# A mixer layer: column-wise small inverse, preparation in three steps, and elementwise work queued behind evacuations

## The chip, the cores and the metric

The kernel runs on one core of a Trainium2 chip. The metric is the device time of one execution in microseconds. Before the change the median of three runs was 3375.29 us (3373.78 to 3380.63).

A core has five engines that work side by side, each through its own queue in order. PE multiplies matrices; PEld is its loading of weights. DVE and POOL do elementwise work, ACT does activation functions and copies, and SP only issues DMAs here. An instruction that waits for another engine's result holds up everything behind it in its own queue.

## The reference

One layer works on 256 latent tokens and 256 context tokens of width 2048, all in float32: a SwiGLU block on both, a token mixer, and a second SwiGLU block on the latent tokens alone, each followed by a residual sum and a layer norm. The change touches the mixer. Half of its width is an RWKV-7 recurrence, with 16 heads of 64 channels, run forwards and backwards; the other half is a gated MLP over chunks of 128 tokens:

```
def token_mixer(h_x, h_c, ...):
    p_x, p_c = h_x @ w_in, h_c @ w_in                       # 2048 -> 3 * 1024 + 256 + 2 * 1024
    r, k, v, w_lo, a_lo, g_lo = split(xs)                   # xs: token-shifted projections
    w     = -softplus(-(w0[d] + tanh(w_lo) @ w_up[d])) - 0.5
    iclr  = sigmoid(a0[d] + a_lo @ a_up[d])
    k_d   = k * (1 + (iclr - 1) * k_a)
    decay = exp(-exp(w))
    # per head and direction d, over tokens t (context first, then latent):
    S_t = S_{t-1} (diag(w_t) + a_t^T b_t) + v_t^T k_t,   y_t = S_t r_t
    out = (group_norm(y) + bonus) * g                       # RWKV half
    gm  = u * (W_s layer_norm(v) + b)                       # gated MLP half
    return concat([out, gm]) @ w_out
```

## The kernel before

Large products are made of three matmuls each (`mm3`, lines 313 to 316), with weights and activations split into a high and a low part. For the weights `wsplit` (line 293) does this: SP loads 512 KB into one of three buffers `raw`, ACT rounds it to `whi` (line 302), and DVE or POOL subtracts to get `wlo` (line 305). There are four buffers of each part.

The recurrence is cut into chunks of 64 tokens. A **unit** is one pair of heads in one direction: 8 pairs times 2 directions make 16 units, numbered 0 to 15. Even units (d = 0) run forwards, odd ones backwards. A unit passes through three chains of steps:

- `begin` (line 1103): for even units a prologue, then `prep` (line 712). From the projections it makes the decays (`pz`, `zp`, the scan `pf`, the exponentials `e`, `ei`), the scaled keys `bk` and receptances `ar`, `ac`, the chunk matrices `aa` by matmuls `px` and a masked copy, transposes `pt` and products `pak`.
- `inverse` (line 858): each 64 x 64 triangular chunk matrix is inverted. `small_inverse` (line 825) collects its 16 x 16 diagonal blocks into `a16` on DVE (line 833), writes them to DRAM (`scr`), and reads them back spread over the partitions as `abc` (1 MB, line 839). `small_steps` (line 845) then makes 15 substitution steps on DVE, each a product with `abc` (line 852) and a reduction (line 853). Four rounds of small matmuls (`pX`, `pR`, twice each) with evacuations on DVE or ACT join the blocks to the whole inverse `R`.
- `finish` (line 1121): `solve` makes `pu`, `pg`, `pq`, and then walks over the 8 chunks: `pS` on PE, the new state `S` on DVE (line 1011), and so on, with outputs `py` and `y`. Backward units add the group norm (`pgn`, line 1072) and the gate (`gup` loaded from DRAM, `pgt`, `epilogue`).

`together` (line 1132) runs `finish` of unit u, `inverse` of u + 1 and `begin` of u + 2 side by side. Every `yield` ends a step; after each round of steps `burst` takes some **project work** from a queue: the large products of the projections of later units (`pp`), of the gated MLP (`pgv`, `pu` with `h` as input) and of the output projection (`pwo`). `pace` sets how much: what is left, over the units left, over `SLOTS`. One step of project work is three matmuls of 256 columns. A scheduler that keeps each engine's program order as the priority, and a model of when inputs are ready, fixes the order of every queue when the program is built; `tc.issue_after(ins)` makes instructions stand behind `ins` on their engine.

Of the kernel before, what the change touches and what calls it, by code (L numbers as in the profile page):

```python
# [38 lines left out]
SLOTS = 13  # L39
# [14 lines left out]
def tile_layer(ctx: ExitStack, tc: tile.TileContext, x, c, ctx_in, c_ctx, w_ada, b_ada, ln_g, ln_b,  # L54
# [89 lines left out]
    mb = const.tile([P, 4], F32, name="mb")  # L144
    for b in range(4):
        nc.vector.tensor_tensor(mb[:, b:b + 1], (bit1 if b >= 2 else bit0)[32], (bit1 if b % 2 else bit0)[16], op=ALU.mult)
# [144 lines left out]


    def wsplit(src, n, by_col=False):

        _, a, b = src.shape
        raw = wp.tile([P, a, b], F32, tag="raw", name="raw", bufs=RAWB)
        nc.sync.dma_start(raw, src)
        parts = []
        for i in range(n):
            r = raw[:, :, b // n * i:b // n * (i + 1)] if by_col else raw[:, a // n * i:a // n * (i + 1), :]  # L300
            hi = wp.tile(list(r.shape), F32R, tag="whi", name="whi", bufs=HIB)
            nc.scalar.copy(hi, r)  # L302
            lo = wp.tile(list(r.shape), F32R, tag="wlo", name="wlo", bufs=HIB)
            turn[0] += 1
            (nc.gpsimd if turn[1] and turn[0] % turn[1] == 0 else nc.vector).tensor_tensor(lo, r, hi.bitcast(F32), op=ALU.subtract)  # L305
            parts.append((hi, lo))
        return parts
# [393 lines left out]

    gl = const.tile([P, T], F32, name="gl")
# [9 lines left out]
    def prep(t, d, k, r, kk, vt, ups, kdx, s):  # L712
# [12 lines left out]
        nc.scalar.activation(ic, pa, AF.Tanh, scale=0.5, bias=a0c)  # L725
        nb = pre("nb")
        nc.vector.scalar_tensor_tensor(nb, ic, 1.0, kk, op0=ALU.add, op1=ALU.mult)

        nc.vector.tensor_reduce(zp[:, :, 0], zp[:, :, 1:L // 2 + 1], axis=AX.X, op=ALU.add, negate=True)
        pf = pre("pf", (P, NCH, L + 1))  # L730
        nc.vector.tensor_tensor_scan(fl(pf), fl(m65), fl(zp), 0.0, op0=ALU.mult, op1=ALU.add)
# [4 lines left out]
        nc.scalar.activation(fl(ei), fl(pf), AF.Exp, scale=-sgn)  # L736
# [3 lines left out]
        wn = own("wn", (P, NCH), bufs=3)  # L740
        if d == 0:
            nc.vector.tensor_tensor(wn[:, 0:7], e[:, 0:7, last], ei[:, 1:8, first], op=ALU.mult)
        else:
            nc.vector.tensor_tensor(wn[:, 1:8], e[:, 1:8, last], ei[:, 0:7, first], op=ALU.mult)
            nc.vector.tensor_tensor(wn[:, 0:1], e[:, 0:1, last], ei[:, 7:8, first], op=ALU.mult)
        ei = ei[:, :, 1:L + 1] if d == 0 else ei[:, :, 0:L]
        ar = pre("ar", (P, 2, 4, L))
# [4 lines left out]
        bk = [pre(f"bk{q}", (P, 4, 2, L)) for q in range(2)]  # L752
        nbv, eiv = (z.rearrange("p (g q) t -> p g q t", q=2) for z in (c64(nb), ei))
        for q in range(2):
            nc.vector.scalar_tensor_tensor(bk[q][:, :, q, :], nbv[:, :, q, :], -0.5, eiv[:, :, q, :], op0=ALU.mult, op1=ALU.mult)
        nc.vector.tensor_tensor(ar[:, 1], c64(r), ecur[:, 4:8], op=ALU.mult)

        kd = pre("kd")
        nc.vector.tensor_scalar(kd, ic, -1.0, kac, op0=ALU.add, op1=ALU.mult)
        nc.vector.scalar_tensor_tensor(kd, kd, 1.0, k, op0=ALU.add, op1=ALU.mult)  # L760
        kdv = c64(kd).rearrange("p (g q) t -> p g q t", q=2)
        for q in range(2):
            nc.gpsimd.tensor_tensor(bk[q][:, :, 1 - q, :], kdv[:, :, q, :], eiv[:, :, q, :], op=ALU.mult)
# [4 lines left out]
        for _ in range(3):  # L768
            yield
# [5 lines left out]
        for half in (1, 0):  # L775
# [16 lines left out]
            for h in range(2):  # L792
# [6 lines left out]
                nc.vector.tensor_tensor(aa[:, :, h, 2 * half:2 * half + 2], pa, mk[0], op=ALU.mult)  # L799
# [9 lines left out]
        for q in range(2):  # L809
# [3 lines left out]
            nc.scalar.copy(fl(bkt[:, q]), pt)  # L813
# [8 lines left out]
        nc.scalar.copy(rhs[:, :, :, 0, :], pt.rearrange("p (g h c) -> p g h c", g=4, h=2))  # L822
        s.update(wn=wn, rt=rt, aa=aa, arm=arm, rhs=rhs, bkt=bkt)

    def small_inverse(d, s):


        a16 = own("a16", (P, 8, 16))
        for b in range(4):
            for q in range(2):  # L830
                qs = slice(64 * q, 64 * q + 64)
                aq = s["aa"][qs, q].rearrange("p h g t -> p (h g) t")
# [3 lines left out]
        scr = dr.tile([P, 128], F32, tag="scr", name="scr")  # L836
        nc.sync.dma_start(scr, fl(a16))
        abc = own("abc", (P, 16, 8, 16))
        nc.sync.dma_start(abc.rearrange("p s j t -> p (s j t)"),
                            scr.rearrange("(g s) c -> g (s c)", g=8).unsqueeze(1).to_broadcast([8, 16, 2048]))  # L840
        return small_steps(d, s, abc)

    behind = [None]

    def small_steps(d, s, abc):
        x = own("x16", (P, 8, 16), bufs=2)
        nc.scalar.copy(x, i16.unsqueeze(1).to_broadcast([P, 8, 16]))
        sub = own("a16", (P, 8, 16))
        for i in (range(1, 16) if d == 0 else range(14, -1, -1)):
            r = slice(0, i + 1) if d == 0 else slice(i, 16)  # L850
            with tc.issue_after(behind[0].ins) if behind[0] is not None and i in (1, 14) else nullcontext():
# [6 lines left out]
    def inverse(d, s):  # L858

        aa = s["aa"]  # L860
        for _ in range(3):
            yield
        yield from s["small"]

        R1 = own("R1", (P, 8, 32))
        nc.vector.tensor_tensor(R1.rearrange("p j (b t) -> p j b t", t=16), s["x16"].unsqueeze(2).to_broadcast([P, 8, 2, 16]),
                                mh[:, 0, :].unsqueeze(1).unsqueeze(3).to_broadcast([P, 8, 2, 16]), op=ALU.mult)
        Rt = own("Rt", (P, 8, 32))
        nc.vector.transpose(Rt, R1)
# [8 lines left out]
        nc.vector.tensor_tensor(Z, pX[:, 0:256].rearrange("p (i t) -> p i t", t=32),  # L878
# [23 lines left out]
        for q in range(2):  # L902
            sb = slice(64 * q + fb, 64 * q + fb + 32)
            pz = pX[sb, 0:256].rearrange("p (i t) -> p i t", t=32)
            if q:
                nc.scalar.copy(Z[sb], pz)
# [8 lines left out]
        for q in range(2):  # L915
            sa = slice(64 * q + fa, 64 * q + fa + 32)
            pz = pR[sa, 0:256].rearrange("p (i t) -> p i t", t=32)
            if q:
                nc.scalar.copy(R[sa, :, fb:fb + 32], pz)
# [4 lines left out]
    def solve(d, s, vt, y):  # L924
# [7 lines left out]
        for half in range(2):  # L932
# [12 lines left out]
            nc.scalar.copy(uv[1][64:128, g2], puv[64:128, :, :, 0, :])  # L945
# [588 lines left out]
```

## Time and profile before

| | us |
|---|---|
| median of three runs | 3375.29 |
| the profiled execution | 3370.43 |
| its span, first to last instruction | 3368.7 |
| PE busy in the span | 3202.2 |
| DVE busy | 2163.8 |
| ACT busy | 1255.9 |
| POOL busy | 436.7 |

The page gives for each engine the time in which it was busy. Its strip of 40 slices shows PE at 9 tenths and more nearly everywhere, except between about 1600 and 2610 us, where slices stand at 7 to 9 and the clock that PE was granted lies at 8 or 9 tenths. The 16 units run in that part, from 1727 to 2572 us. A busy PE there isn't a PE at its peak: matmuls are pipelined, and each counts as busy until its result is out.

### The profile page before, as it was taken

The numbers are of one execution on the slowest core, as the hardware profiler recorded it, in microseconds if no ns is written. First come the engines' busy times: TensorE is split into PE (matmuls) and PEld (weight loads), VectorE is DVE, ScalarE is ACT, GpSimd is POOL, SyncE is SP. The second block draws the span as 40 slices with busy tenths as digits, with TensorE's granted clock in tenths as the row PEclk, the third lists the DMA queues.
The fourth block names the chain that finished last, engine by engine and source line by source line (L and its number), as shares of the span: only waits on it lengthen the run. The fifth ranks groups of instructions, "written<-read, shape, count | busy, mean of one in ns | idle before, by whom it ended". The sixth has DMA issues, their size and how long they took to land. (4 is left out here: it accounts for less than half of the span.)

```text
span 3368.7 us, 55611 instructions
## 1 busy us (share of the span) xinstructions
PE 3202.2 (95%) x21224; PEld 2548.5 (76%) x21224; DVE 2163.8 (64%) x4425; ACT 1255.9 (37%) x2205; POOL 436.7 (13%) x393
## 2 busy tenths in 40 slices
PE   8999999999999999999798989888889999999997
PEld 4556877777877887888787777777678888888886
DVE  3345677967566566443967777877677756656567
ACT  2321222222222222222564454444333554444443
POOL 2100000000000000000553232323223000000003
PEclk9999999999999999999898899998899999999999
DMA  9866464756656556333354253444453665555554
GB/s 302 266 198 204 142 187 150 218 176 221 194 159 225 159 181 201 120 95 106 119 162 116 73 123 88 108 100 107 124 117 124 221 209 193 190 191 188 188 189 148
DMA packets 546387, 554.35 MB, mean 165 GB/s; under 512 B 24207, under 2 KB 399156, under 8 KB 544072
## 3 DMA queue, kind: packets, MB, share of 16 engines
q1 hardware_dynamic: 545672, 550.61, 53.3%
q8 instruction: 167, 2.74, 0.3%
q14 instruction: 100, 0.82, 0.1%
q0 software_dynamic: 384, 0.17, 0.0%
q10 hardware_dynamic: 64, 0.02, 0.0%
HBM read 543.35 MB, written 7.35 MB: 163 GB/s over the span
## 5 line engine op out<-in xcount | busy, mean ns | idle before, releaser
L302 ACT CAST whi<-raw 128x512 fp32r<-128x512 f32 (+1 forms) x1366 | 840.1, 618 | 1717.9 <-PE po L315 356.0
L305 DVE TENSOR_TENSOR wlo<-raw,whi 128x512 fp32r<-128x512 f32 (+1 forms) x1188 | 833.4, 704 | 630.8 <-ACT whi L302 621.1
L305 POOL TENSOR_TENSOR wlo<-raw,whi 128x512 fp32r<-128x512 f32 x178 | 242.5, 1365 | 2565.2 <-ACT whi L302 2518.2
L314 PE MATMUL po<-ahi,whi 128*128 128x512 f32 (+1 forms) x768 | 292.4, 381 | 2.8 <-DVE X L420 2.2
L316 PE MATMUL po<-ahi,wlo 128*128 128x512 f32 (+1 forms) x768 | 290.4, 378 | 4.6 <-DVE wlo L305 4.6
L315 PE MATMUL po<-alo,whi 128*128 128x512 f32 (+1 forms) x768 | 291.7, 380 | 0.0
L314 PE MATMUL pgate<-h,whi 128*128 128x512 f32 x704 | 277.9, 395 | 1.8 <-ACT h L310 1.2
L314 PE MATMUL pup<-h,whi 128*128 128x512 f32 x704 | 278.0, 395 | 0.9 <-ACT whi L302 0.9
L316 PE MATMUL pup<-h,wlo 128*128 128x512 f32 x704 | 275.2, 391 | 1.0 <-DVE wlo L305 0.9
L316 PE MATMUL pgate<-h,wlo 128*128 128x512 f32 x704 | 275.1, 391 | 0.8 <-DVE wlo L305 0.6
L315 PE MATMUL pgate<-h,whi 128*128 128x512 f32 x704 | 274.7, 390 | 0.0
L315 PE MATMUL pup<-h,whi 128*128 128x512 f32 x704 | 274.5, 390 | 0.0
L420 DVE SCALAR_TENSOR_TENSOR X<-po,modc,X 128x256 f32<-128x256 f32 x352 | 155.0, 478 | 154.6 <-PE po L316 149.4
L277 DVE SCALAR_TENSOR_TENSOR vt<-xk,wa,vt 128x512 f32<-128x512 f32 x256 | 186.9, 746 | 28.7 <-DMA xk<-in_w_ada_dram 26.7
L277 DVE SCALAR_TENSOR_TENSOR vt<-xv,wa,vt 128x512 f32<-128x512 f32 x224 | 163.5, 746 | 24.1 <-DMA xv<-in_w_ada_dram 22.6
L314 PEld LDWEIGHTS po<-ahi,whi 128*128 128x128 f32 x768 | 145.4, 189 | 42.4 <-issue 7.0
L314 PEld LDWEIGHTS pgate<-h,whi 128*128 128x128 f32 x704 | 132.1, 188 | 53.5 <-ACT whi L302 11.5
L315 PEld LDWEIGHTS po<-alo,whi 128*128 128x128 f32 x768 | 145.6, 190 | 35.0 <-issue 7.5
L316 PEld LDWEIGHTS po<-ahi,wlo 128*128 128x128 f32 x768 | 145.5, 189 | 34.2 <-DVE wlo L305 5.3
L314 PEld LDWEIGHTS pup<-h,whi 128*128 128x128 f32 x704 | 132.2, 188 | 51.7 <-ACT whi L302 13.2
L314 PE MATMUL pp<-h,whi 128*128 128x256 f32 (+1 forms) x448 | 164.6, 367 | 3.3 <-ACT whi L302 2.3
L316 PE MATMUL pp<-h,wlo 128*128 128x256 f32 (+1 forms) x448 | 157.0, 351 | 7.2 <-DVE wlo L305 4.3
(389 smaller groups left out, 6323.9 us busy)
## 6 DMA issues: line engine op xcount, KB each, us to landing
raw<-in_ffn_b_wi_dram SPq DMA_DIRECT2D x176, 512.0 KB
raw<-in_ffn_a_wi_dram SPq DMA_DIRECT2D x156, 512.0 KB
xv<-in_w_ada_dram SPq DMA_DIRECT2D x256, 256.0 KB
xk<-in_w_ada_dram SPq DMA_DIRECT2D x256, 256.0 KB
raw<-in_w_in_dram SPq DMA_DIRECT2D x110, 512.0 KB
raw<-in_ffn_a_wo_dram SPq DMA_DIRECT2D x96, 512.0 KB
raw<-in_ffn_b_wo_dram SPq DMA_DIRECT2D x88, 512.0 KB
abc<-scr SPq DMA_DIRECT2D x16, 1024.0 KB
```

What stands on the lines that cost most here:

```text
L277: nc.vector.scalar_tensor_tensor(acc[v], raw, csil[:, kt, v:v + 1], acc[v], op0=ALU.mult, op1=ALU.add)
L302: nc.scalar.copy(hi, r)
L305: (nc.gpsimd if turn[1] and turn[0] % turn[1] == 0 else nc.vector).tensor_tensor(lo, r, hi.bitcast(F32), op=ALU.subtract)
L314: nc.tensor.matmul(o, wh, ah, start=start, stop=False)
L315: nc.tensor.matmul(o, wh, al, start=False, stop=False)
L316: nc.tensor.matmul(o, wl, ah, start=False, stop=stop)
L420: nc.vector.scalar_tensor_tensor(xs, po[:, sl], gc[:, d:d + 1], xs, op0=ALU.mult, op1=ALU.add)
```

## The change

Outside the mixer one constant (`mb`) goes, and the rest of the program stays. In the mixer:

- The 16 x 16 blocks are no longer collected on DVE. Eight DMAs per unit write them from `aa` to `scr`, in runs of 16 numbers, and `abc` is read inside `prep` instead of after the round.
- The substitution goes by columns: the product reads `abc` in runs of neighbours, without the diagonal, and `sub` starts as the identity on ACT.
- `prep` is cut into three steps, with the DVE's part of each behind the last evacuation noted in `urgent`; `kd` is made before `bk`, and POOL takes `bk` before `ar` and `ac`.
- `inverse` starts one step earlier and has one more step between the transposed block and `pX`. `begin` comes before `inverse` in each round.
- `whi` and `wlo` on ACT and DVE stand behind the evacuations of the round before.
- Both norms become two operations over all groups; that of the gated MLP moves into `gmlp_u`; the group norm has one more step, and `gup` is loaded in the fifth step of `solve`.
- `SLOTS` is 12 instead of 13.

```diff
-SLOTS = 13
+SLOTS = 12
...
+    def queued(ins):
+        return tc.issue_after(ins.ins) if ins is not None else nullcontext()
...
-            nc.scalar.copy(hi, r)
+            with queued(before[1]):
+                nc.scalar.copy(hi, r)
...
-            (nc.gpsimd if turn[1] and turn[0] % turn[1] == 0 else nc.vector).tensor_tensor(lo, r, hi.bitcast(F32), op=ALU.subtract)
+            with queued(before[0]):
+                (nc.gpsimd if turn[1] and turn[0] % turn[1] == 0 else nc.vector).tensor_tensor(lo, r, hi.bitcast(F32), op=ALU.subtract)
...
+    def behind():
+
+        return queued(urgent[0])
...
+        with behind():
+            nc.vector.tensor_reduce(zp[:, :, 0], zp[:, :, 1:L // 2 + 1], axis=AX.X, op=ALU.add, negate=True)
+            nc.vector.tensor_tensor_scan(fl(pf), fl(m65), fl(zp), 0.0, op0=ALU.mult, op1=ALU.add)
+        yield
...
+        with behind():
+
+            nc.vector.tensor_scalar(kd, ic, -1.0, kac, op0=ALU.add, op1=ALU.mult)
+            nc.vector.scalar_tensor_tensor(kd, kd, 1.0, k, op0=ALU.add, op1=ALU.mult)
+            nc.vector.scalar_tensor_tensor(nb, ic, 1.0, kk, op0=ALU.add, op1=ALU.mult)
+        yield
...
+        scr = dr.tile([P, 128], F32, tag="scr", name="scr")
+        for q in range(2):
+            for b in range(4):
+                rows = slice(64 * q + 16 * b, 64 * q + 16 * b + 16)
+                nc.sync.dma_start(scr[rows, :].rearrange("p (j t) -> p j t", t=16),
+                                  aa[rows, q].rearrange("p h g t -> p (h g) t")[:, :, 16 * b:16 * b + 16])
         yield
...
-                nc.vector.scalar_tensor_tensor(a16[qs], aq[:, :, 16 * b:16 * b + 16], mb[qs, b:b + 1],
-                                               a16[qs] if b else i16[qs].unsqueeze(1).to_broadcast([64, 8, 16]),
-                                               op0=ALU.mult, op1=ALU.add)
...
-                nc.vector.tensor_tensor(sub[:, :, r], x[:, :, r], abc[:, r, :, i].rearrange("p s j -> p j s"), op=ALU.mult)
-            nc.vector.tensor_reduce(x[:, :, i], sub[:, :, r], axis=AX.X, op=ALU.add)
-            if i % 4 == 0:
+            with behind():
+                nc.vector.tensor_tensor(sub[:, :, lo:hi], x[:, :, lo:hi], s["abc"][:, i, :, lo:hi], op=ALU.mult)
+                nc.vector.tensor_reduce(x[:, :, i], sub[:, :, r], axis=AX.X, op=ALU.add)
+            if n % 4 == 3:
                 yield
...
+        nc.vector.transpose(R1, Rt)
+        yield
         yield
         pX = ps_v("pX")
...
-                nc.vector.scalar_tensor_tensor(Sn, pS[:, 0:64], wn[:, cc:cc + 1], wc[:, g, q, :], op0=ALU.mult, op1=ALU.add)
+                urgent[0] = nc.vector.scalar_tensor_tensor(Sn, pS[:, 0:64], wn[:, cc:cc + 1], wc[:, g, q, :], op0=ALU.mult, op1=ALU.add)
...
+            if d == 1 and n == 4:
+                gup = sol("gup", (P, P))
+                nc.sync.dma_start(gup, g_up[0, :, P * t:P * t + P])
...
         while chains:
+            before[:] = urgent
             for ch in list(chains):
                 if next(ch, chains) is chains:
                     chains.remove(ch)
             burst()
+        before[:] = [None, None]
```

How the queues move shows in the order of instructions, which is fixed before anything runs. Three places follow.

DVE in unit 4, around the states `S` of its first chunks; `a` and `x` are the product and the unknowns of the substitution for unit 5, `nb`, `zp`, `pf` belong to the preparation of unit 6. Before:

```order
L1011 SCALAR_TENSOR_TENSOR S<-pS,wn,wc 128x64
L852 TENSOR_TENSOR a_17833<-x_17831,abc 128x8x2
L305 TENSOR_TENSOR wlo<-raw,whi 128x512
L853 TENSOR_REDUCE x_17831<-a_17833 128x8
L727 SCALAR_TENSOR_TENSOR nb<-ic,kk 128x512
L852 TENSOR_TENSOR a_17833<-x_17831,abc 128x8x3
L729 TENSOR_REDUCE zp<-zp 128x8
L853 TENSOR_REDUCE x_17831<-a_17833 128x8
L1011 SCALAR_TENSOR_TENSOR S<-pS,wn,wc 128x64
L852 TENSOR_TENSOR a_17833<-x_17831,abc 128x8x4
L731 SCALAR_TENSOR_TENSOR pf<-m_96,zp 128x520
```

Now:

```order
L856 TENSOR_TENSOR a_17871<-x_17870,abc 128x8x8
L857 TENSOR_REDUCE x_17870<-a_17871 128x8
L737 TENSOR_REDUCE zp<-zp 128x8
L1016 SCALAR_TENSOR_TENSOR S<-pS,wn,wc 128x64
L738 SCALAR_TENSOR_TENSOR pf<-m_96,zp 128x520
L856 TENSOR_TENSOR a_17871<-x_17870,abc 128x8x9
L309 TENSOR_TENSOR wlo<-raw,whi 128x512
L857 TENSOR_REDUCE x_17870<-a_17871 128x8
L666 SCALAR_TENSOR_TENSOR xr<-pp,mus,xr 128x4x63
```

The substitution is at its eighth step where it was at its third, `nb` has left this place, and the scan `pf` stands directly behind a state.

PE at the end of unit 3: `pgn` transposes its output for the group norm, and `pR` is the last round of the inverse of unit 4; `pgv` is project work. Before:

```order
L314 MATMUL pgv<-whi,h_12726 128x256
L315 MATMUL pgv<-wlo,h_12726 128x256
L316 MATMUL pgv<-whi,h_12727 128x256
L314 MATMUL pgv<-whi,h_12734 128x256
L315 MATMUL pgv<-wlo,h_12734 128x256
L316 MATMUL pgv<-whi,h_12735 128x256
L1076 MATMUL pgn<-ident,y 128x128 x2
L914 MATMUL pR_17510<-R_17240,Z 32x32 x16
L314 MATMUL pgv<-whi,h_12786 128x256
```

Now:

```order
L890 MATMUL pR<-R_17329,Z 32x32 x32
L1013 MATMUL py<-qy,S 64x64 x2
L1072 MATMUL pb<-kdx,bones 128x256
L1044 MATMUL pn<-bones,sq 128x2 x4
L904 MATMUL pX_17560<-Rt,aa 32x32 x16
L1081 MATMUL pgn<-ident,y 128x128 x2
L919 MATMUL pR_17596<-R_17329,Z 32x32 x16
L1053 MATMUL prn<-ident,rb 128x128 x4
L1060 MATMUL ptv<-ident,xv 64x128
L1097 MATMUL pgb<-ident,y 128x128 x2
L1100 MATMUL pgt<-gl,gup 128x256
L944 MATMUL pu<-rhs,R 64x128 x16
```

The project work that stood between the rounds of the inverse is gone from here; 96 project matmuls' worth of 256 columns, 32 steps, stand right behind this `pu` of unit 4. Over units 0 to 10 together 349 such steps lie between a unit's `pu` and its `pq`, where 103 lay, and in the rest of a unit some 27 where some 46 lay; in the later units they are spread about as before.

SP around the transfers for the inverse of unit 4; `raw` are weight loads. Before:

```order
L297 DMA raw<-in_w_in_dram 128x4x256
L837 DMA scr<-a_16913 128x128
L297 DMA raw<-in_w_in_dram 128x4x256
L839 DMA abc<-scr 128x1x2048
L297 DMA raw<-in_w_in_dram 128x4x256
L1090 DMA gup<-in_g_up_dram 128x128
```

Now:

```order
L299 DMA raw<-in_w_in_dram 128x4x256
L1224 DMA gscr<-gu 128x256
L830 DMA scr<-aa 128x1x16 x8
L842 DMA abc<-scr 128x1x2048
L299 DMA raw<-in_w_in_dram 128x4x256 x4
L1131 DMA gup<-in_g_up_dram 128x128
```

One transfer to `scr` became eight, none of the weight loads stands between them and `abc` any more, and `gup` follows four weight loads later.

## Rows read from the trace of the kernel before

**Rows 1.** Four stretches of the span: up to the mixer, its first part, the 16 units, the rest. Columns: length, busy us of each engine with its number of instructions, granted clock as a share, DMA share, GB/s.

```profile
0.00:1600.00 1600.00, 1576.05 (x6905) 1193.59 (x6906) 924.85 (x1638) 426.04 (x714) 40.64 (x49) 1.00 0.59 184
1600.00:1727.00 127.00, 108.06 (x811) 103.06 (x809) 103.18 (x194) 72.66 (x149) 76.62 (x67) 0.92 0.49 147
1727.00:2572.00 845.00, 750.04 (x10034) 619.11 (x10033) 620.48 (x1790) 374.50 (x706) 267.95 (x236) 0.91 0.42 107
2572.00:3368.70 796.70, 768.09 (x3480) 632.75 (x3478) 515.34 (x806) 382.68 (x639) 51.52 (x42) 0.98 0.57 188
```

**Rows 2.** What PE waited for in the stretch of the units: waiting line, line waited for, us in total, times, longest.

```profile
PE pgt L1096 <- DMA gup<-in_g_up_dram: 11.5, 3, 8.0
PE pX L875 <- DVE Rt L869: 11.0, 9, 2.6
PE pS L1004 <- DVE a L852: 10.7, 2, 6.2
PE pq L982 <- DVE wc L975: 9.1, 5, 2.6
PE px L789 <- DVE aa L799: 8.7, 5, 2.7
PE px L789 <- POOL bk L763: 8.2, 8, 2.2
PE pgv L315 <- DVE wlo L305: 4.7, 4, 2.2
PE pa L718 <- DVE kk L1050: 4.3, 1, 4.3
PE pR L914 <- DVE Z L908: 3.6, 2, 2.9
PE pgb L1093 <- DVE y L1084: 3.1, 5, 1.1
```

**Rows 3.** The timeline of DVE and PE around the first `pX` of one unit: start, us, engine, line, what, and in brackets the wait before it.

```profile
1973.72 0.47 DVE L662 SCALAR_TENSOR_TENSOR xv<-pp,mus,xv 128x255 f32<-128x255 f32 x1
1974.11 0.41 DVE L866 TENSOR_TENSOR R<-x,mh 128x256 f32<-128x256 f32 x1
1974.44 0.47 DVE L662 SCALAR_TENSOR_TENSOR xv<-pp,mus,xv 128x252 f32<-128x252 f32 x1
1974.83 0.43 DVE L869 STREAM_TRANSPOSE Rt<-R 128x256 f32<-128x256 f32 x1
...
1975.41 1.08 PE L875 MATMUL pX<-Rt,aa 32*32 32x32 f32 x64 [1.74 <-DVE Rt L869]
```

**Rows 4.** Waits of DVE in the same stretch, in the columns of rows 2.

```profile
DVE nb L727 <- ACT ic L725: 32.3, 10, 7.3
DVE o L1098 <- PE pgt L1096: 17.8, 3, 11.3
DVE a L852 <- DMA raw<-in_w_in_dram: 5.8, 1, 5.8
DVE a L852 <- DMA abc<-scr: 5.5, 2, 4.5
```

**Rows 5.** The way of one unit's blocks to DVE: the last `aa`, the last `a16`, SP's two transfers, and the first product with `abc`. Columns as in rows 3.

```profile
1966.99 0.41 DVE L799 TENSOR_TENSOR aa<-px,ma 128x256 f32<-128x256 f32 x1
...
1995.43 0.35 DVE L833 SCALAR_TENSOR_TENSOR a<-aa,mb,a 64x128 f32<-64x128 f32 x1
1995.81 0.34 SPq L837 DMA_DIRECT2D scr<-a  x1
...
1997.86 0.62 SPq L839 DMA_DIRECT2D abc<-scr  x1
...
2014.97 0.18 DVE L852 TENSOR_TENSOR a<-x,abc 128x16 f32<-128x16 f32 x1 [4.54 <-DMA abc<-scr]
```

**Rows 6.** The longest wait of `pS`: the engines' timelines, columns as in rows 3.

```profile
2516.44 0.28 PE L315 MATMUL pwo<-h,whi 128*128 128x256 f32 x1
2516.56 0.28 PE L316 MATMUL pwo<-h,wlo 128*128 128x256 f32 x1
2523.01 0.48 PE L1004 MATMUL pS<-S,gi 64*64 64x64 f32 x4 [6.17 <-DVE a L852]
...
2524.22 0.41 PE L314 MATMUL pwo<-h,whi 128*128 128x256 f32 x1
2524.43 0.41 PE L315 MATMUL pwo<-h,whi 128*128 128x256 f32 x1
...
2519.68 0.76 DVE L311 TENSOR_TENSOR h<-ol,h 128x256 fp32r<-128x256 f32 x2 [7.55 <-ACT h L310]
```

**Rows 7.** Groups of DVE and POOL instructions in the stretch of the units: line, engine, operation, names, shapes, number, busy us and mean ns, and idle time before them.

```profile
L305 DVE TENSOR_TENSOR wlo<-raw,whi 128x512 fp32r<-128x512 f32 x116 | 98.1, 847 | 21.3 <-ACT whi L302 20.4 <-issue 0.2
L833 DVE SCALAR_TENSOR_TENSOR a<-aa,mb,a 64x128 f32<-64x128 f32 x96 | 39.1, 407 | 2.7
L833 DVE SCALAR_TENSOR_TENSOR a<-aa,mb,i 64x128 f32<-64x128 f32 x32 | 11.5, 359 | 0.5
L1014 DVE TENSOR_TENSOR y<-py,qy 128x64 f32<-128x64 f32 x64 | 13.6, 213 | 5.8 <-PE py L1008 5.7
L972 DVE TENSOR_TENSOR gi<-pg,i 128x256 f32<-128x256 f32 x32 | 13.3, 415 | 14.6 <-PE pg L968 14.5
L1171 DVE TENSOR_SCALAR gz<-gz,gmv,grs 128x64 f32<-128x64 f32 x32 | 8.5, 336 | 7.7 <-POOL grs L530 7.7
L1084 DVE TENSOR_SCALAR y<-pgn,gnmv,gnrs 128x64 f32<-128x64 f32 x28 | 7.7, 337 | 6.3 <-POOL gnrs L530 6.3
L891 DVE TENSOR_TENSOR R<-R,mh 128x512 f32<-128x512 f32 x16 | 10.9, 679 | 0.0
...
L305 POOL TENSOR_TENSOR wlo<-raw,whi 128x512 fp32r<-128x512 f32 x116 | 159.4, 1376 | 397.7 <-ACT whi L302 354.6 <-PE py L1008 21.8 <-issue 6.6
```

**Rows 8.** The timeline of DVE, one product of 120 numbers by `abc` (compare the one of 16 in rows 5); and the waits of SP's queue for free buffers in the stretch of the units, in the columns of rows 2.

```profile
1971.92 0.37 DVE L852 TENSOR_TENSOR a<-x,abc 128x120 f32<-128x120 f32 x1
...
SPq L297 <- DVE wlo L305: 269.6, 84, 12.6
SPq L297 <- POOL wlo L305: 211.4, 69, 9.9
```

More of the change, by code (lines that the diff above doesn't have):

```diff
@@ L290, in tile_layer @@
     turn = [0, 0]
+    urgent, before = [None, None], [None, None]
+    def queued(ins):
+        return tc.issue_after(ins.ins) if ins is not None else nullcontext()
     def wsplit(src, n, by_col=False):
@@ L750, in prep @@
         nc.gpsimd.tensor_tensor(ac, c64(kk)[:, 0:4], eprev[:, 0:4], op=ALU.mult)
[L752 to L763, printed above, removed]
+        wn = own("wn", (P, NCH), bufs=3)
+        with behind():
+            for q in range(2):
+                nc.vector.scalar_tensor_tensor(bk[q][:, :, q, :], nbv[:, :, q, :], -0.5, eiv[:, :, q, :], op0=ALU.mult, op1=ALU.mult)
+            nc.vector.tensor_tensor(ar[:, 1], c64(r), ecur[:, 4:8], op=ALU.mult)
+            if d == 0:
+                nc.vector.tensor_tensor(wn[:, 0:7], e[:, 0:7, last], eif[:, 1:8, first], op=ALU.mult)
+            else:
+                nc.vector.tensor_tensor(wn[:, 1:8], e[:, 1:8, last], eif[:, 0:7, first], op=ALU.mult)
+                nc.vector.tensor_tensor(wn[:, 0:1], e[:, 0:1, last], eif[:, 7:8, first], op=ALU.mult)
         if d == 0:
@@ L767, in prep @@
             nc.gpsimd.tensor_tensor(kdx, kdx, kd[:, T:W2], op=ALU.add)
-        for _ in range(3):
+        for _ in range(2):
             yield
@@ L838, in small_inverse @@
         abc = own("abc", (P, 16, 8, 16))
         nc.sync.dma_start(abc.rearrange("p s j t -> p (s j t)"),
[L840 to L845, printed above, removed]
+                          scr.rearrange("(g s) c -> g (s c)", g=8).unsqueeze(1).to_broadcast([8, 16, 2048]))
+        s.update(wn=wn, rt=rt, aa=aa, arm=arm, rhs=rhs, bkt=bkt, abc=abc)
+    def small_inverse(d, s):
@@ L846, in small_steps @@
         x = own("x16", (P, 8, 16), bufs=2)
[L847 removed]
         sub = own("a16", (P, 8, 16))
[L849 to L854 removed]
+        for z in (x, sub):
+            nc.scalar.copy(z, i16.unsqueeze(1).to_broadcast([P, 8, 16]))
@@ L860, in inverse @@
         aa = s["aa"]
-        for _ in range(3):
+        for _ in range(2):
             yield
-        yield from s["small"]
+        yield from small_inverse(d, s)
+        Rt = own("Rt", (P, 8, 32))
+        nc.vector.tensor_tensor(Rt.rearrange("p j (b t) -> p j b t", t=16), s["x16"].unsqueeze(2).to_broadcast([P, 8, 2, 16]),
+                                mh[:, 0, :].unsqueeze(1).unsqueeze(3).to_broadcast([P, 8, 2, 16]), op=ALU.mult)
         R1 = own("R1", (P, 8, 32))
[L866 to L869, printed above, removed]
+        nc.vector.transpose(R1, Rt)
+        yield
         yield
@@ L1116, in begun @@
             ups[t + 1] = load_ups(t + 1)
-        unit[u]["small"] = small_inverse(d, unit[u])
         if d == 1:
@@ L1194, in gmlp_u @@
         pt = ps_g("pu1")
-        yield from gemm(ub + P * j, T, W2, pt)
+        for n, w in enumerate(gemm(ub + P * j, T, W2, pt)):
+            if n == 2 and j % 2 == 0:
+                gmlp_norm(j // 2)
+            yield w
         for i in range(2):
@@ L1287, in tile_layer @@
     gens[1, 2] = put(project(1, 2))
-    together(inverse(0, unit[0]), begin(1))
+    together(begin(1), inverse(0, unit[0]))
     begun(1)
@@ L1304, in tile_layer @@
         chains = [finish(u)]
-        if u + 1 < nu:
-            chains.append(inverse((u + 1) % 2, unit[u + 1]))
         if u + 2 < nu:
@@ L1311, in tile_layer @@
             chains.append(begin(u + 2))
+        if u + 1 < nu:
+            chains.append(inverse((u + 1) % 2, unit[u + 1]))
         together(*chains)
```

94 lines of the change are left out of this document (43 added, 51 removed).

## The prediction

> **What bounds the kernel now.** I read the table of stretches first. The change touches only the mixer, and of its parts only the 16 units leave PE much to gain: in their 845 us PE is busy for 750.0, so it waits for 95 us, and its clock was granted at 0.91 on the mean. The first and last stretches have the full clock or nearly so, and their work isn't edited [rows 1]. With two levels, 1 and 0.5, a mean of 0.91 means that (1 - 0.91) / 0.5 x 845 = 152 us ran at the lower one. The next view is what PE waited for: no single cause, but ten lines that make 74.9 of the 95 us, nearly all on results of DVE, on one DMA (`gup`), and on POOL's `bk` [rows 2]. DVE is busy for 620 us, 73% of the stretch, so it isn't full; but its queue is in order, and what PE wants stands behind other work. The timeline shows it: `Rt`, which `pX` waits 1.74 us for, ran between two `xv` operations of 0.47 us that nobody was in a hurry for [rows 3]. DVE also stood still itself, for 32.3 us at `nb` behind ACT's `ic`, 17.8 at `o` and 11.3 in two waits of the product `a` [rows 4]. So the bound is PE, plus chains of short hops between PE and a DVE whose queue is badly ordered.
>
> **The change, part by part.** I add everything to the profiled execution, 3370.43 us (span 3368.7, 1.7 around it). The median of the runs, 3375.29, lies 4.9 above it, and I add that at the end. What a measurement can tell from no change is about 0.2%, 6.75 us.
>
> *DVE's work.* The 128 copies into `a16` (39.1 + 11.5 = 50.6 us) go. The two norms (8.5 + 7.7 = 16.2 us) become, per unit, two operations: the nearest rows of such sizes are 0.415 us for 256 columns and 0.679 for 512, about 0.8 a unit, 13 us, so 3 go [rows 7]. The product by columns reads neighbours. By rows a product of 120 numbers took 0.37 us and one of 16 took 0.18, which is 1.8 ns a number [rows 5, 8]; contiguous operations of 64 and 256 columns differ by (0.415 - 0.213) / 192 = 1.05 ns [rows 7]. Per unit 15 products of together 1080 numbers become 960, about 1 us less, so 15 us in all. The sum is 69 us off DVE, 11%. None of this is on PE's path by itself; it pays only where PE waits for DVE.
>
> The two-input halves of the new norms meet POOL's long casts. POOL's `wlo` took 1376 ns, DVE's 847 on the mean [rows 7]. The Trainium skill (SBUF — State Buffer, section "Who interferes with whom") says that a DVE instruction with two SBUF inputs and a GpSimd instruction that reads SBUF block each other for a whole instruction; the trace agrees in so far as DVE's own two-input casts are uneven. By that rule, as an estimate, 16 new operations could each lose up to 1.4 us, and DVE would be spared 47 us, not 69; my forecast would stay, and the slower rival below would cost 15 us more.
>
> *PE's waits for DMA and for the blocks.* `gup` is loaded many steps ahead, so its 11.5 us go. For one unit the last `aa` was ready at 1967.4, but the last `a16` was done at 1995.8, because eight copies stood in DVE's queue; `abc` was issued at 1997.9 and used at 2015.0, 17 us later, after DVE had waited 4.54 us [rows 5]. Now `scr` goes out right behind `aa` and nothing stands between it and `abc`, so `abc` comes some 20 us sooner and the substitution starts before it is wanted. I take off what `pS` waited behind the product: 10.7 - 6.2 = 4.5 us. The 6.2 were not the product's: DVE sat at `h` behind ACT for 7.55 us [rows 2, 6], and this stays. Seven more issues on SP per unit cost 7 x 16 x 0.34 to 0.62 = 38 to 69 us of its queue [rows 5], hidden by 481 us in which SP waits for free buffers [rows 8]; without that cover the weights would be later by 2.4 to 4.3 us a unit.
>
> The new pieces of `scr` are runs of 16 numbers, 64 bytes, and no transfer in the rows has such runs. The Trainium skill (DMA: Bandwidth & Descriptors, section "Specifications") wants 512 bytes or more for line rate; by it the way to `abc` would be longer than I think. No run here shows that; if it ate the whole lead of 20 us, the 4.5 us would stay and the sum would be 3320.
>
> *PE's waits for DVE's queue.* `Rt` has one more step before `pX`, and `prep` stands behind the last evacuation, so of 11.0 us I take 8. `wc`, `aa`, `kk`, `Z` and `y` make 9.1 + 8.7 + 4.3 + 3.6 + 3.1 = 28.8 us [rows 2]; they are late for the queue and the stalls in it, which are now 69 us of work and up to 61.4 us of waiting less [rows 4]. Bounds 0 and 28.8; I take three quarters, 22, since each of these waits is short (longest 4.3) and the stall at `nb` alone was up to 7.3. `bk` now comes first on POOL: half of 8.2, 4 us. Together 11.5 + 4.5 + 8 + 22 + 4 = 50.
>
> *The clock.* It falls after waits: project matmuls came every 0.12 us before the wait of 6.17 us and every 0.21 after it [rows 6]. One us at the lower level thus costs 0.43 us of matmul work. If half of the waits go, I let half of the 152 us go, 77: upper 77 x 0.43 = 33 us. The project work (1032 steps by the count in the code) of 3 x 0.12 = 0.36 us, is 372 of the 750 busy us; if only that half quickens, 16. I take 24.
>
> *What is added.* Casts now stand behind evacuations. The bounds are nothing and 116 x 0.847 = 98 us, where each cast of DVE [rows 7] makes PE wait for its length; now PE waits 4.7 us for a `wlo` [rows 2], so they run ahead and I take +5. ACT's `whi` moves likewise and is in that number; behind a held cast stand only later casts and evacuations of the next round. The second addition is seen in the order alone: in units 0 to 10, 349 - 103 = 246 project steps, 88 us, move to between `pu` and `pq`, because the casts they need come later. The hops they used to cover stand bare. The bounds are 0 and 88 us; I take +10, as those hops mostly have the other chains, `begin` and `inverse`, beside them.
>
> Sum: -50 - 24 + 5 + 10 = -59, so 3311, and on the scale of the median **3316 us**.
>
> **Rivals.** *Everything goes.* All waits but the 6.2 of ACT and the 4.7 of the casts go, 84 us, and the clock stays up (152 us at 0.21 to 0.43 would be 32 to 65; I take 40, near the lower, as hops of one result stay): 3370.4 - 124 + 4.9 = 3251. For it: each wait in rows 2 has an edit. Against it: PE's hops remain in number, and PE waits another 20 us in small pieces that no row of ten names.
>
> *Half given back.* The gains of 74 stand, but casts and bare hops cost a quarter of their bounds, (98 + 88) / 4 = 46: -28, so 3347. For it: 32 steps in one pile behind `pu` of unit 4 where none of them is needed to cover anything.
>
> *Slower.* Place: `pq` to the next `pu` in units 0 to 10. If DVE and the hops set the length there, taking 88 us of project work out doesn't shorten it, and the pile behind `pu` adds 88. DVE's lighter work gives back 69 x 11/16 = 47 and `gup` 11.5: +29.5, so 3405. It decides from the point where DVE and hops are longer than what PE has left. Against it: of 11/16 x 845 = 581 us, PE keeps 581 - 88 = 493, and DVE's work is 11/16 x 620 - 47 = 380; the hops would have to add 113 us or more. For it: the forward chain of `S` alternates strictly, PE and DVE, and each result also has a way to travel.
>
> *Nothing comes of it.* The waits move to whatever now stands at the front of the queues (`pf`, the product behind an evacuation), and the clock with them: 3375 within 7. Against it: `a16` and `gup` are really gone.
>
> **How the numbers follow.** Forecast 0.50, everything goes 0.15, half given back 0.15, slower 0.15, nothing 0.05. The likeliest's own range is 3285 to 3340: DVE's waits at 28.8 and the clock at 33 give 16 us less, `bk` and `Rt` whole 7 less, the rest of the small waits some 8; the other way the DVE term at half (8), the clock at 16 (8) and the additions 8 higher. The range goes from 3245, which takes in the first rival, to 3385, which takes in the third and the last and leaves out most of the slower one. Faster by over 0.2%: the first three, 0.80; within it 0.05; slower 0.15.
>
> **What would show it.** In the changed profile the waits of `pgt` on `gup` and of `nb` on `ic` should be gone, `a` on `abc` too; DVE's busy time in the units should fall by about 69 us, PE's waits from 95 to 45 to 60, and the granted clock rise from 0.91 to about 0.95. PE's waits for `wlo` should stay under 10 us. If between `pq` and the next `pu` of units 0 to 10 PE shows many short waits for `S`, `R` or `aa` at a lower clock, the bare hops are dear and the slower rival has it; if waits for `wlo` or `whi` lead the list, the casts were held too long. I am wrong if the units take 845 us or more, or if the time comes from stretches outside them.

## The result, and the profile after

The changed kernel takes 3418.89 us (median of 4 runs, 3413.43 to 3426.02) against 3374.53 for the kernel before (4 runs): a ratio of 1.0134, 95% interval 1.0116 to 1.0152. It is 44 us slower; 3316 was forecast, and the range ended at 3385. The profiled execution has a span of 3424.3 us, 55.6 more than before.

The stretches of the changed kernel, in the columns of [rows 1]:

```profile
0.00:1600.00 1600.00, 1572.96 (x6835) 1187.66 (x6836) 919.23 (x1624) 422.88 (x710) 36.78 (x46) 0.99 0.59 184
1600.00:1727.00 127.00, 107.04 (x793) 101.93 (x792) 102.97 (x191) 70.40 (x145) 75.31 (x66) 0.92 0.47 143
1727.00:2572.00 845.00, 724.52 (x9539) 608.69 (x9538) 542.81 (x1552) 374.73 (x710) 268.10 (x232) 0.89 0.42 104
```

In the same 845 us PE is now busy for 724.5 instead of 750.0, at a clock of 0.89 instead of 0.91: it waits more, not less, and at their end it isn't through with the units. DVE did get lighter. To see where the time went I cut the trace at the first `pu` of unit 0, at that of unit 11 and behind the last `pgt`. The kernel before, from 1600 us on:

```profile
1600.00:1790.50 190.50, 162.48 (x1410) 148.52 (x1408) 151.29 (x305) 103.11 (x202) 100.03 (x87) 0.91 0.46 131
1790.50:2339.10 548.60, 491.60 (x6668) 397.56 (x6667) 417.34 (x1224) 253.05 (x473) 181.44 (x161) 0.91 0.42 105
2339.10:2574.60 235.50, 206.48 (x2788) 178.19 (x2787) 156.89 (x461) 91.47 (x180) 64.33 (x56) 0.92 0.43 115
```

The changed kernel:

```profile
1600.00:1814.90 214.90, 173.26 (x1477) 159.97 (x1475) 152.34 (x298) 105.42 (x206) 100.46 (x88) 0.85 0.43 120
1814.90:2412.70 597.80, 518.54 (x6787) 431.14 (x6787) 380.80 (x1117) 267.11 (x500) 194.10 (x168) 0.89 0.39 99
2412.70:2626.40 213.70, 191.24 (x2691) 165.31 (x2691) 146.53 (x422) 86.79 (x175) 62.43 (x55) 0.92 0.49 121
```

The start is 24 us longer and has a clock of 0.85; units 0 to 10 are 49 longer, the last five 22 shorter, since more project work was done before them. Cut further at each `pq`, units 0 to 10 spend 183 us between `pu` and `pq` (94 before) and 415 from `pq` to the next `pu` (454 before): the pile of project work adds 89, near the 88 of its 246 steps, and the rest of those units is only 40 shorter, for the missing project work, DVE's lighter queue and the sooner `gup` together. Unit 4 shows the pile. Before, then now:

```profile
1994.80:2003.00 8.20, 8.20 (x130) 7.13 (x129) 6.32 (x19) 5.03 (x10) 2.36 (x2) 1.00 0.81 200
```

```profile
2035.90:2053.90 18.00, 18.00 (x164) 15.34 (x163) 5.10 (x12) 5.18 (x11) 4.04 (x3) 0.93 0.44 115
```

PE is never idle in either, but DVE works for 5.1 of the 18 us where it worked for 6.3 of the 8.2: little else goes on beside the pile.

The waits of PE from 1727 to 2640 us, since the units now end later, in the columns of [rows 2]:

```profile
PE pS L1009 <- DVE S L1016: 14.2, 12, 2.7
PE px L801 <- DVE wn L772: 11.1, 2, 8.3
PE prn L1053 <- ACT rb L1049: 10.7, 6, 2.6
PE pu L318 <- ACT wsT L1207: 7.8, 4, 4.0
PE px L801 <- DVE x L857: 7.7, 3, 6.0
PE pgv L319 <- DVE wlo L309: 6.0, 5, 3.1
...
PE pX L880 <- DVE Rt L870: 4.1, 5, 1.2
...
PE px L801 <- DVE aa L811: 2.6, 3, 0.9
...
PE pq L987 <- DVE wc L980: 1.1, 1, 1.1
```

Each wait that the prediction took as a gain did shrink: `gup` and `bk` are gone, `Rt` fell from 11.0 to 4.1, `aa` from 8.7 to 2.6, `wc` from 9.1 to 1.1. Others stand in their places: `S`, `wn`, `rb`, `wsT`; and those for `wlo` grew (`pgv`: 4.7 to 6.0). DVE's stalls at `nb`, `o` and the raw load are gone too [rows 4], but the front of its queue is now somewhere else:

```profile
DVE wlo L309 <- ACT whi L305: 84.6, 33, 5.4
DVE gi L977 <- PE pg L973: 38.4, 9, 10.4
DVE zp L737 <- ACT zp L731: 24.9, 8, 6.3
```

The products of the substitution on DVE in the kernel before, from 1600 to 2640 us, in the columns of [rows 7]:

```profile
L852 DVE TENSOR_TENSOR a<-x,abc 128x16 f32<-128x16 f32 (+14 forms) x240 | 98.0, 408 | 14.9 <-DMA raw<-in_w_in_dram 5.8 <-DMA abc<-scr 5.5
```

The groups of the changed kernel that answer to them and to the norms of [rows 7], same stretch:

```profile
L856 DVE TENSOR_TENSOR a<-x,abc 128x8 f32<-128x8 f32 (+14 forms) x240 | 89.3, 372 | 4.0 <-DMA abc<-scr 1.5
...
L1091 DVE TENSOR_TENSOR y<-y,gnrs 128x256 f32<-128x256 f32 x8 | 4.4, 553 | 4.8 <-POOL gnrs L534 4.8
L1090 DVE TENSOR_TENSOR y<-pgn,gnmv 128x256 f32<-128x256 f32 x8 | 3.3, 409 | 0.0
L1186 DVE TENSOR_TENSOR gz<-gz,gmv 128x512 f32<-128x512 f32 x4 | 3.2, 803 | 0.0
L1187 DVE TENSOR_TENSOR gz<-gz,grs 128x512 f32<-128x512 f32 x4 | 2.7, 679 | 0.0
```

### The profile page after: what moved, and what is told of

Read it like the earlier page. It is cut to its first block, busy times and chain, and to the rows that moved or that the text cites. A ratio compares the mean times of both kernels' runs of the same rounds, so it can differ in the third digit from the quotient of the medians.

```text
span 3424.3 us, 55542 instructions
## 1 busy us (share of the span) xinstructions
PE 3221.7 (94%) x21224; PEld 2574.4 (75%) x21224; DVE 2110.2 (62%) x4253; ACT 1263.3 (37%) x2225; POOL 442.0 (13%) x393
```

## The experiments

All were timed in three rounds beside the kernel before, whose median lay between 3375.1 and 3378.0. Two theories stood first. **P**: the project work that lands in a pile behind `pu`, and is missing over the hops of the chains, is the cost; where it is put follows from the held casts and SLOTS. A pile is what lies between a unit's `pu` and its `pq`. **Q**: the three-slot preparation and the held elementwise work make the chains themselves longer.

### Undoing one part of the change

e1 frees the casts, e2 sets SLOTS back, e3 does both, e4 takes away the waiting of preparation, substitution and norm.

```diff
e1, e3:  -            before[:] = urgent
         +            before[:] = [None, None]
e2, e3:  -SLOTS = 12
         +SLOTS = 13
e4:      -        return queued(urgent[0])        # behind()
         +        return nullcontext()
```

> The changed kernel, but the casts of the weights don't stand behind evacuations. In its order 265 project steps lie between pu and pq of units 0 to 10 (349 in the changed kernel, 103 before) and 84 ahead of unit 0 (64 and 82). Theory P (the pile behind pu is what costs, 0.36 us a step, and the start loses the 20 steps that were its cover): 84 x 0.36 = 30 us in units 0 to 10 and some 15 at the start come back, so about 3375. Theory Q (the three-slot preparation and the held elementwise work make the chains longer, the pile is only where project work lands): 3410 to 3420, nothing comes back but a few us of waits for casts.

> The changed kernel with SLOTS 13 instead of 12. Its order has 206 project steps between pu and pq of units 0 to 10 instead of 349, and 55 steps more are left for the units after the tenth. Theory P: 143 x 0.36 = 51 us come back in units 0 to 10, of which 55 x 0.36 = 20 go again in the later units: about 3388. Theory Q: the length of the chains in units 0 to 10 doesn't change; 3410 to 3425.

> Both: casts free and SLOTS 13; 171 project steps between pu and pq of units 0 to 10, 84 ahead of unit 0. Theory P: 178 x 0.36 = 64 us less in units 0 to 10, 15 less at the start, some 15 more later: about 3355, faster than the kernel before. Theory Q: 3405 to 3420.

> The changed kernel, but preparation, substitution and norm on DVE don't stand behind the last evacuation (the casts still do). The pile stays, 347 steps. Theory P: within 10 us of the changed kernel, 3410 to 3430. Theory Q: the held work was what lengthened the chains; 3385 to 3400.

Measured: e1 3359.0 (ratio to before 0.9952, 0.9937 to 0.9968), e2 3395.0 (1.0057, 1.0039 to 1.0076), e3 3358.8 (0.9945, 0.9925 to 0.9964), e4 3459.4 (1.0242, 1.0220 to 1.0264).

Free casts give back 60 us, more than the whole loss and more than the 45 of P. SLOTS gives 24 with the casts held and nothing without. Q falls: it left e1 to e3 at 3405 and more. The work behind evacuations is not what hurts: without it the kernel is 40 us slower still, against both theories; the product of the substitution now gets to the front of DVE's queue before its data are there. DVE in e4:

```profile
DVE a L856 <- DMA abc<-scr: 115.3, 15, 11.1
```

In the changed kernel this wait is 1.5 us (groups above). e1 by the same cuts, unit 0 to the end of unit 10, then the last five:

```profile
1797.70:2355.90 558.20, 492.58 (x6787) 406.42 (x6786) 379.25 (x1117) 267.50 (x500) 188.33 (x165) 0.93 0.42 105
2355.90:2559.60 203.70, 183.14 (x2691) 158.64 (x2691) 142.97 (x424) 88.26 (x174) 60.15 (x54) 0.95 0.51 128
```

PE does the same 6787 matmuls in units 0 to 10 as in the changed kernel, in 558 us instead of 598, and the start is 17 us shorter. DVE still stands 85.2 us at `wlo` behind ACT's `whi` in e1, so that row, the longest of the changed kernel, isn't where the 60 us are.

What a held cast does can be read at the start, in unit 0's preparation. ACT in the changed kernel:

```profile
1726.93 0.62 ACT L305 CAST whi<-raw 128x512 fp32r<-128x512 f32 x1
...
1746.77 0.41 ACT L777 COPY kdx<-kd 128x256 f32<-128x256 f32 x1 [0.85 <-DVE kd L749]
1748.74 0.41 ACT L786 COPY ra<-ar 128x256 f32<-128x256 f32 x1 [1.57 <-DVE ar L769]
1754.58 0.59 ACT L820 COPY rhs<-pt 128x512 f32<-128x512 f32 x1 [5.43 <-PE pt L819]
...
1758.20 0.59 ACT L840 COPY rhs<-pak 128x512 f32<-128x512 f32 x1 [1.33 <-PE pak L839]
1758.68 0.62 ACT L305 CAST whi<-raw 128x512 fp32r<-128x512 f32 x1
```

ACT in e1:

```profile
1741.81 1.13 ACT L305 CAST whi<-raw 128x512 fp32r<-128x512 f32 x2
1742.84 0.40 ACT L777 COPY kdx<-kd 128x256 f32<-128x256 f32 x1
1743.15 0.62 ACT L305 CAST whi<-raw 128x512 fp32r<-128x512 f32 x1
1743.80 0.41 ACT L786 COPY ra<-ar 128x256 f32<-128x256 f32 x1
1744.11 0.61 ACT L305 CAST whi<-raw 128x512 fp32r<-128x512 f32 x1
1750.17 0.59 ACT L820 COPY rhs<-pt 128x512 f32<-128x512 f32 x1 [5.45 <-PE pt L819]
```

In e1 four casts run around the copies `kdx` and `ra`, before which ACT waits for 0.85 and 1.57 us in the changed kernel; before `rhs` it waits as long in both. Held, the next `whi` comes only behind the last copy of the chain, and for 31 us, from 1727.55 to 1758.68, there is no cast. PE has nothing to put over the hop and stands, in the changed kernel:

```profile
1749.30 2.08 PE L801 MATMUL px<-ar,bk 64*128 64x128 f32 x16 [8.28 <-DVE wn L772]
```

In e1 `px` waits for `wn` 1.1 us at most in this part, though 5.1 for an `aa`; all listed waits of PE from 1727 us to the first `pu` make 21.6 us in the changed kernel and 14.0 in e1. The weight buffers stay full meanwhile: when SP has issued `abc`, the next load still waits for a cast of POOL.

```profile
SPq L299 <- POOL wlo L309: 3.0, 1, 3.0
```

So the transfers stop as well; windows of the changed kernel, columns as in [rows 1]:

```profile
1745.00:1763.00 18.00, 12.54 (x110) 10.40 (x110) 8.51 (x16) 8.02 (x16) 4.01 (x5) 0.62 0.07 11
1763.00:1777.00 14.00, 9.80 (x62) 9.30 (x62) 12.53 (x22) 4.43 (x9) 8.78 (x9) 0.83 0.92 170
```

That is 11 GB/s for 18 us, with the clock at 0.62, and then a rush at 0.92 of the DMA engines.

### Which half of the cast, and in company of what

e5 holds only `wlo`, e6 only `whi`; e7 puts the held casts alone into the kernel before (with notes of the evacuations, as the change has them), e8 the sooner `gup` alone.

```diff
e5:  -            with queued(before[1]):     # whi
     +            with nullcontext():
e6:  -            with queued(before[0]):     # wlo
     +            with nullcontext():
e7 (on before):  +            before[:] = urgent
                 +            with queued(before[1]): ...
                 +            with queued(before[0]): ...
e8 (on before):  +            if d == 1 and n == 4:
                 +                gup = sol("gup", (P, P))
```

> The changed kernel, but of the casts only wlo (DVE, POOL) stands behind evacuations; whi on ACT is free. Its order still has 341 project steps between pu and pq of units 0 to 10, and 76 ahead of unit 0 (64 in the changed kernel, 84 with both free). Theory P (the project work that lands in the pile and is missing elsewhere is the cost): only some 10 us of the start and 3 of the pile come back, 3400 to 3410. Theory A (ACT's held whi is the cost, since wlo and the matmuls wait for it): about 3365, as with both free.

> The counterpart: whi on ACT held, wlo free; 348 steps between pu and pq and 64 ahead of unit 0. Theory P: as the changed kernel, 3412 to 3425. Theory D (DVE's held wlo is the cost, a cast in time but behind a state in DVE's queue): about 3365.

> The kernel before with this one edit: the casts held behind the evacuations of the round before. 129 project steps between pu and pq of units 0 to 10 (103 before), 64 ahead of unit 0 (82). Theory P: 25 x 0.36 = 9 us and the start some 15, so about 3400. A rival: the held casts cost their 60 us whatever else is there, about 3435; the other rival, that they only hurt in company of the changed chains: within 7 us of 3376.

> The kernel before with this one edit: gup loaded in the fifth step of solve. The order of PE is nearly that of before (113 steps in the piles). If the wait of 11.5 us was on the path, 3365; if another wait takes its place (the chain behind pgt is waited for anyway), 3372 to 3380.

Measured: e5 3403.2 (1.0075, 1.0050 to 1.0101), e6 3413.6 (1.0099, 1.0068 to 1.0130), e7 3401.5 (1.0070, 1.0045 to 1.0096), e8 3358.2 (0.9942, 0.9926 to 0.9958).

P had e5, e6 and e7 right to within its numbers. Either half held is nearly as bad as both: 44 and 55 of the 60 us stay, which fits that a matmul step wants both parts. In the kernel before, where it leaves 129 steps in the piles, the same edit costs 24 us; in the changed kernel, with 349, it costs 60. `gup` alone brings 20 us (14 to 25), more than its waits of 11.5 [rows 2]; between the two profiled executions it is 12.

### What the other edits bring with free casts

e9 adds to e8 the direct blocks and the columns. e10 is e3 with the preparation in one slot; e11 is e1 with SLOTS 14; e12 is the kernel before with SLOTS 12.

```diff
e9 (on before with gup sooner):
-        small_inverse: eight products into a16, one scr, abc
+        eight scr from aa, abc inside prep; sub[:, :, lo:hi] = x * abc[:, i, :, lo:hi]
e10 (on e3):  -        yield      # the two inside prep
              -        for _ in range(2):
              +        for _ in range(3):
e11 (on e1):  +SLOTS = 14
e12 (on before):  +SLOTS = 12
```

> The kernel before with gup sooner (as in e8) and the blocks written from aa straight to DRAM, abc read inside the preparation, the substitution by columns; no other edit. If DVE's lighter queue (66 us less) and the earlier abc take waits of PE away, as the prediction has it for 4.5 us of abc and a good part of 28.8 + 11: 3330 to 3345. If PE's waits only move, since each hop of a chain ends in a wait for something: 3352 to 3362, as e8 (3358).

> As e3 (the changed kernel, casts free, SLOTS 13), and the preparation in one slot again, still behind the last evacuation, with three empty steps as before. One step less in begin; 109 project steps in the piles of units 0 to 10 instead of 171. Theory P: 62 x 0.36 = 22 us less than e3, about 3337. If the three slots themselves brought something (DVE no longer at the head of its queue waiting for ACT): 3365 or more.

> The changed kernel, casts free, SLOTS 14; 109 project steps in the piles of units 0 to 10 against 265 in e1, and 51 more after the tenth unit. Theory P: 156 x 0.36 = 56 less, 18 more later: 3321. e1 and e3 speak against its size (95 steps made no difference): if the casts cost by holding back project work and not by the pile's length, 3350 to 3360.

> The kernel before with SLOTS 12 alone; 155 project steps in the piles of units 0 to 10 (103), 25 steps less after the tenth unit. Theory P: 51 x 0.36 = 18 more, 9 less: about 3386. If the pile's length costs nothing by itself: 3370 to 3380.

Measured: e9 3345.1 (0.9896, 0.9875 to 0.9916), e10 3370.0 (0.9977, 0.9961 to 0.9993), e11 3352.3 (0.9924, 0.9899 to 0.9948), e12 3387.6 (1.0025, 1.0012 to 1.0038).

e9 is 13 us below e8: the direct blocks and the columns pay, by a quarter of the 54 us of DVE work that they save (2164.6 to 2110.4 us in the whole program). e12 is slower by 10 where P had 9. But e11 and e10 fall against P. With free casts, piles of 265, 171 and 109 steps (e1, e3, e11) give 3359, 3359 and 3352, and e10 has 109 at 3370. The length of the pile alone is not the price; P holds where the casts are held, and as a measure of SLOTS in the kernel before. e10 against e3 says that three slots are worth 11 us there, with intervals that just touch.

Where the time went shows in the cuts used above, in us, one profiled execution of each (that of e11 is 9 us above its median):

| | 1600 us to the first `pu` | `pu` to `pq`, units 0 to 10 | `pq` to the next `pu` | the last five units |
|---|---|---|---|---|
| before | 190.5 | 94 | 454 | 236 |
| changed | 214.9 | 183 | 415 | 214 |
| e1, casts free | 197.7 | 148 | 410 | 204 |
| e3, and SLOTS 13 | 196.1 | 129 | 417 | 220 |
| e11, and SLOTS 14 | 193.7 | 99 | 445 | 227 |
| e7, before with casts held | 204.3 | 106 | 459 | 237 |

Held casts cost 17 us at the start, 35 in the piles, 5 in the rest of those units and 10 in the last five (changed against e1), and 14, 12, 4 and 1 in the kernel before (e7). So they cost mainly by longer piles and a later start; the rest of the units, with less project work in it, is hardly longer. With free casts a shorter pile is given back: from e1 to e11 the piles lose 49 us, the rest of those units takes 35 and the last five 23.

### What takes back the rest

e13 is e9 with three slots and the work behind evacuations, e16 the same with SLOTS 14. e14 and e15 undo on e11 the new place of the gated norm, and the inverse's edits (start, extra step, place behind `begin`). e17 puts the inverse's edits alone on e9, e18 on e13.

```diff
e14 (on e11):  -            if n == 2 and j % 2 == 0:
               -                gmlp_norm(j // 2)
e15 (on e11):  -        for _ in range(2):
               +        for _ in range(3):       # inverse
               -        yield                    # behind transpose(R1, Rt)
               +        together(finish, inverse, begin)
e17 (on e9), e18 (on e13): the same the other way round
```

> e9 (the kernel before with gup sooner and the direct blocks by columns, 3345) with the preparation in three slots and it and the substitution behind the last evacuation; kd ahead of bk; casts free, SLOTS 13, no other edit. 134 project steps in the piles of units 0 to 10 instead of 103. If three slots help as e3 against e10 had it (11 us): 3334. If the added step and the longer pile cost as the theory of the pile has it (31 x 0.36 = 11): 3345 to 3356.

> e11 (changed kernel, casts free, SLOTS 14, 3352) with the norm of the gated MLP back behind its gelu, still as two operations. In e11 PE waits 10.4 us for POOL's gz, a line that the kernel before doesn't have. If the norm's new place costs them: 3338 to 3344. If another wait takes the place: 3348 to 3356.

> e11 with the inverse started one step later, without the added step between the transposed block and pX, and ahead of begin in each round, as in the kernel before. If these are what takes back the 7 us between e9 and e11: 3340 to 3346. If the extra step is worth the 8 us that the prediction took for Rt: 3358 to 3362.

> e13 with SLOTS 14: 100 project steps in the piles of units 0 to 10 instead of 134, about 31 more in their rest, 2 more later. Theory P: 33 x 0.36 = 12 less than e13. If e13 is no worse for its pile, the same as e13 within 7.

> e9 (3345) with the inverse started one step earlier, one more step between the transposed block and pX, and begin ahead of inverse in each round; preparation in one slot, casts free, SLOTS 13. e15 against e11 gave 25 us for these edits. If they are worth it alone: 3320 to 3335. If only together with the three slots, whose DVE work they make room for: 3340 to 3350.

> e17 with the preparation in three slots and it and the substitution behind evacuations (so e13, 3353, with the inverse's edits). If the three slots cost 8 us here too: 8 more than e17. If they and the inverse's edits help each other: at or below e17, and 20 to 25 below e13, 3328 to 3335.

Measured: e13 3353.2 (0.9946, 0.9926 to 0.9965), e14 3342.9 (0.9901, 0.9871 to 0.9931), e15 3377.2 (1.0010, 0.9990 to 1.0030), e16 3355.1 (0.9938, 0.9918 to 0.9958), e17 3347.0 (0.9917, 0.9886 to 0.9947), e18 3351.2 (0.9934, 0.9908 to 0.9961).

e14 fits the norm's new place as a loss of 9 us, though the intervals of e11 and e14 overlap: in e11 PE waits for POOL's half of it, and in e14 this wait is gone.

```profile
PE pu L1217 <- POOL gz L1192: 10.4, 3, 7.1
```

The inverse's edits are worth 25 us beside the rest of the change (e15 against e11), and nothing on e9 or e13 (e17, e18). e15 came out above both of its expectations, and e18 at neither of its own. Three slots cost 8 on e9 (e13) and bring 11 beside the rest (e10). Neither fits a fixed price per edit. e9 and e14 have the lowest medians, 1.0% under the kernel before and 2.2% under the changed one (3345.1 and 3342.9 against 3418.9); their intervals don't tell them apart, nor from e17's.

## Why the prediction was wrong

- *The held casts, +5, were the failing step.* They cost 60 us (e1), 24 alone in the kernel before (e7). "They run ahead" was read from PE's waits of 4.7 us for a `wlo` (8.1 with the rows below the ten shown); but in unit 0's preparation they ran ahead because they were free to use ACT's gaps. The term's upper bound of 98 us held it; I chose the end near nothing, and the range of the whole then ended at 3385. Nor was the bound's mechanism right, a PE that waits for each cast: its listed waits for `wlo` from 1727 to 2640 us are 17 us, more than the 10 set as a sign, but 52 of the 69 us between the profiled executions of the changed kernel and e1 stand in the later start and the longer piles.
- *The gains, -74, failed as well*, and by nearly as much: the miss is 103 us, and the casts make 55 of it. With free casts the sum would be 64 under the kernel before (-50 - 24 + 10); e1 is 18 under it, and no run is more than 35. `gup` gave 20 and the blocks with the columns 13 (e8, e9); the rest of the 74 came in no run.
- *The bare hops, +10.* The place and the sign were seen in the order, 246 steps, and the slower rival was built on it with 88 us of pile and 58 given back; the trace shows 89 and 40. Its time, 3405, was nearest, but it had a chance of 0.15, and in part it is luck: it lacked the start, 24 us longer, and the last units, 22 shorter. I argued against it that PE keeps 493 us while DVE needs 380, but the 581 us of that sum hold the piles too: from `pq` to the next `pu` it was 454, and is now 415, in which PE is busy for 338 and DVE for 317, so that neither alone sets the length. The steps move there not only "because the casts they need come later": of the 246, freeing the casts takes 84 away and SLOTS 13 takes 143 (the orders of e1 and e2), so that the two terms aren't independent, and the second is more SLOTS than casts.
- *SLOTS had no term of its own.* It costs 10 us in the kernel before (e12) and 24 with held casts (e2).
- *PE's waits, -50.* `gup` was right in kind and too small (11.5; 20 measured). The other waits shrank as named and came back under other names: PE's idle time in the 845 us is 103 in e1 (845 - 742.0, at 0.94 of the clock) and 120 in the changed kernel, against 95. So the 22 for DVE's queue, the 8 for `Rt` and the 4 for `bk` were sums over waits that are not a sum. The row for the 845 us of e1:

```profile
1727.00:2572.00 845.00, 742.03 (x10194) 621.52 (x10193) 577.17 (x1657) 392.03 (x739) 280.94 (x246) 0.94 0.45 112
```

- *The clock, -24.* It rose to 0.94 with free casts, as forecast (0.95), while the waits stayed; in the changed kernel it fell to 0.89. So PE's idle time alone doesn't tell the clock.
- *DVE's work, -69, was right in kind and came to 54* (2163.8 to 2110.2 us in the whole program): the 128 copies are gone (50.6), the products took 89.3 instead of 98.0, and the norms 13.6, where 13 was estimated from rows; about 62 in these. The term of the columns was mis-sized, 9 for 15. Some 8 us went again in rows for which the sum had nothing, such as DVE's `ar` (615 to 825 ns on the mean) and `bk` (607 to 729); no run shows why. The up to 22 us by the Trainium skill's rule (SBUF — State Buffer, section "Who interferes with whom") don't show in the norms.
- *`abc` sooner was right*: DVE waits 1.5 us for it instead of 5.5. Together with the copies that went and the columns it gave 13 us (e9), where 4.5 was priced for it and a good part of the 22 for DVE's lighter queue.
- *Nothing comes of it* fell (gup, e8), and so did *everything goes*: no median came under 3342.

Open stays why the inverse's edits and the three slots pay beside the rest of the change (e10, e15) and not on the kernel before, alone or together (e13, e17, e18), and why the gains of DVE's lighter queue didn't come. The waits alone don't tell, and no run took the order of one engine while leaving the others.

## What to carry to other kernels

Filler work on engines that take their queues in order added its whole length here where it lay in one pile, and little where it lay over hops, as long as these had room: before holding back its inputs (casts, loads), see whether the engine that makes them idles at the very places where they ran. A list of waits can't be added up as a gain: take one away and measure, as with `gup`, and expect the next hop to show the same wait under another name. Where an order is fixed by a program, count the filler on both sides of each hop before and after, and put the price at the bound's far end unless the cover is seen.

## What the runs showed of the hardware

Eight small issues on SP took longer than eight times the one before. SP in the changed kernel, unit 0:

```profile
1753.99 5.16 SPq L830 DMA_DIRECT2D scr<-aa  x8
1760.67 0.66 SPq L842 DMA_DIRECT2D abc<-scr  x1
```

That is 0.65 us each, where one `scr` took 0.34 [rows 5] and the prediction's bounds for one more ended at 0.62, and 6.7 us from the first `scr` to `abc` where it was 2.1. And they stand at the front of SP's queue until `aa` is there, with the weight loads behind them:

```profile
SPq L830 <- DVE aa L811: 24.6, 1, 24.6
```

This longest wait is at the start, where the next load had to wait for a buffer in any case; with free casts (e1) no wait of `scr` there is over 7.9 us.
